# S5 taps side by side in DRAM, chunk tokens numbered backwards, gate loads pinned, GLU operand cast earlier, in a one-core encoder layer on Trainium2

## The chip, the cores and the metric

The kernel runs on one core of one Trainium2 chip, as one launch. The metric is the device time of an execution in microseconds; lower is better. The kernel before was run three times and took 880.37, 882.69 and 883.11 us (median 882.69).

## The reference

One encoder layer over 512 tokens of width 1024, all in float32. The part that matters here is the mixer: a projection feeds an S5 state-space branch (bidirectional, 32 groups of 16 channels with 64 states each) and a gMLP branch, and both are merged by sigmoid gates. Memory attention and a SwiGLU feed-forward layer follow.

```python
def s5_branch(xa, lam_re, lam_im, log_step, b_re, b_im, c_re, c_im, d, w_glu):
    u = xa.astype(f32).reshape(bsz, seq, S5_GROUPS, S5_GROUP).transpose(1, 0, 2, 3)
    y = d.astype(f32).reshape(S5_GROUPS, S5_GROUP) * u
    for direction, reverse in ((0, False), (1, True)):
        y = y + s5_scan(u, ..., reverse)
    y = jax.nn.gelu(y.transpose(1, 0, 2, 3).reshape(bsz, seq, S5_WIDTH))
    y = y * jax.nn.sigmoid(y @ w_glu.astype(f32))
    return y.astype(xa.dtype)

def reference(...):
    memn = rms_norm(mem, mem_norm_g)
    n = rms_norm(h, mix_norm_g[i])
    proj = n @ w_in[i]
    ya = s5_branch(xa, ...)
    yb = sgu_branch(zu, zv, ...)
    merged = gate_a * (ya @ w_proj_a[i]) + gate_b * (yb @ w_proj_b[i])
    h = h + merged @ w_out[i]
    h = h + memory_cross_attention(...)
    h = h + swiglu(...)
    return rms_norm(h, final_norm_g)
```

## The kernel before

**Matmuls in three parts.** A float32 product is made of three fp32r matmuls: each operand is split into a high part (a cast on ScalarE, line 85) and a low part (a subtraction on VectorE, line 86). `feat`, `tokm` and `product` (line 1143) run these; `feat` and `tokm` go through `mm3` (line 358). Weights come in blocks of 512 KB by a written-out plan: a block is loaded on the SyncE queue three blocks ahead (`wraw`), split two ahead (`whi`, `wlo`), and each of the three buffers exists three times. So the load of a block waits until the block three places ahead of it has been split, and the split until the block three places ahead of it has been multiplied.

**Side work.** The S5 branch is a generator, `s5_program`, that is advanced by `tick` between the matmul blocks of the main work; `later(n, fn)` puts a step off. `finish_side` runs out what is left of it. After recording, a scheduler orders each engine's instructions by a simulated timeline; instructions wrapped in `in_order` keep their program order among each other.

**S5.** The 512 tokens are 64 chunks of Q = 8 tokens. Within a chunk the result is a convolution with 15 lags, from 7 ahead to 7 behind; between chunks a scan over 64 states carries on. The groups are worked off in four octets o of GO = 8 groups. `s5_kernels(o)` makes the taps: `products` multiplies them on TensorE (pk), `store` copies them from PSUM to `ks` and adds the skip term, `spill` writes them to DRAM (`kd`, one row of 15 x 16 values for each group and input channel; four DMAs on SyncE, four on GpSimd), and `load` reads them back as the matrix `tt` (line 855), one DMA for each of the eight tokens l of a chunk, on the partitions l, l + 8, and so on. For the octets 2 and 3 the state matrices e are spilled too (`ed`) and `reload` (line 861) brings both back as soon as octet o - 2 has released the buffers. `s5_outputs(o)` then multiplies: for each group one matmul with the taps (py<-tt,u) and two with the states (py<-e,ss), line 941; `emit` copies the result (yn), `turn_y` transposes it (pyt), and `put` applies GELU (y, line 962) and stores it to DRAM (`yd`, line 965). There is one buffer for y.

**The end of the mixer.** While the octets end, the main work multiplies the second gate (its sigmoids go to `part`, line 1171) and then the gMLP projection by w_proj_b as 14 block products of a seven-product scheme (`b_product`, lines 1208 to 1243; names bx, bv, bq, x1, v1). `seed` (qv, line 1156) copies a product into a second PSUM bank, and the next product is added there; `kept` (u, line 1161) saves one before it is added to. After the last block product, `finish_side` ends S5 and closes its pool; a new pool holds the GLU's operand: `ygt` is loaded from `yd` (line 1255), cast (`yg_hi`, line 1256) and subtracted (`yg_lo`, line 1257). Two `feat` blocks multiply it by w_glu; `glu_evac` takes the sigmoid and multiplies (glu, line 1265) and splits into `ya`. The gains g_mem and g_x (line 471) and the gates `gat` (line 1279, four loads of 512 KB from `gad`, three buffers) are loaded next, and four `feat` blocks multiply `ya` by w_proj_a; `pa_evac` multiplies by the gate and adds `part`. Every load named here is issued by SyncE, in one queue, in order: a load that waits holds those behind it.

Of the kernel before, what the change touches and what calls it, by code (L numbers as in the profile page):

```python
# [9 lines left out]
F32 = mybir.dt.float32  # L10
F32R = mybir.dt.float32r
AF = mybir.ActivationFunctionType
ALU = mybir.AluOpType
# [39 lines left out]
def hybrid_layer_kernel(  # L53
# [566 lines left out]
    def s5_setup():  # L620
# [89 lines left out]
        for src in (pr, pi):  # L710
            pe = s5p.tile([P, G, Q], F32, name="pe%d" % len(st["pe"]))
            pw = s5p.tile([P, G, Q], F32, name="pw%d" % len(st["pw"]))
            A_.copy(pe[lo_], src[lo_, :, 0:Q])
            V.tensor_copy(pe[hi_], src[hi_, :, 0:Q][:, :, ::-1])
            V.tensor_copy(pw[lo_], src[lo_, :, 1:Q + 1][:, :, ::-1])
            A_.copy(pw[hi_], src[hi_, :, 1:Q + 1])
            st["pe"].append(pe)
            st["pw"].append(pw)
        ca = s5p.tile([P, 2, G], F32, name="ca")
# [55 lines left out]
    def lc(t, g):  # L775
        return t[:, g].rearrange("p a b -> p (a b)")
# [4 lines left out]
    def s5_kernels(o):  # L781
# [43 lines left out]
            later(0.5, lambda: store(ps))  # L825

        def store(ps):
            ks = s5p.tile([P, 2, P], F32, tag="y", name="ks")
            dd = s5p.tile([P, 2, C], F32, tag="dd", name="dd", bufs=2)
            in_order(V.tensor_tensor(dd, st["dmask"].unsqueeze(1).to_broadcast([P, 2, C]),  # L830
                                     st["dcol"][:, 2 * o:2 * o + 2].unsqueeze(2).to_broadcast([P, 2, C]), ALU.mult))
            nc.scalar.copy(ks, ps)
            V.tensor_tensor(ks[:, :, 0:C], ks[:, :, 0:C], dd, ALU.add)
            later(0.5, lambda: spill(ks))

        def spill(ks):
# [12 lines left out]
    ed = {o: dp.tile([2, P, GO * Q * C], F32, name=f"ed{o}") for o in (2, 3)}  # L849

    def load(o, es):
        tt = s5p.tile([P, GO, P], F32, tag=("tt", "raw_c")[o % 2], name="tt")
        kf = st["kd", o].rearrange("g c l e -> c g (l e)")
        for l in range(Q):
            nc.sync.dma_start(tt[l::Q], kf[:, :, (7 - l) * C:(15 - l) * C])  # L855
        st["oct", o] = (es[0], es[1], tt)

    def reload(o):
# [60 lines left out]
    def s5_outputs(o):  # L919
# [12 lines left out]
        def mix_():  # L932
            ps = aux("py", (P, 4, 2, 4, C))
            ks = (0, 1, 2) if o in ed else (1, 2, 0)
            for h in range(4):
                for k in ks:
                    for j in range(2):
                        g = 4 * j + h
                        a = u[:, o * GO + g, :] if k == 0 else ss[:, k - 1, g, :]
                        b = (tt[:, g, :], lc(e_re, g), lc(e_im, g))[k]  # L940
                        in_order(nc.tensor.matmul(ps[64 * j:64 * j + 64, :, :, h, :].rearrange("p q d c -> p d q c"), a,
                                                  b.rearrange("p (d q c) -> p d q c", d=2, q=4),
                                                  start=k == ks[0], stop=k == ks[2], tile_position=(0, 64 * j)))
            later(1, lambda: emit(ps))
            if o + 2 in ed:
                later(0.5, lambda: reload(o + 2))
# [283 lines left out]
    b_product(x1, 1, 6)  # L1230
    u1 = zf[0][:, :, T0]
    nc.scalar.copy(u1, x1)
    b_product(bq, 0, 3)
    gated(0, 1, T0, minus(bq, u2))
    b_product(x1, 1, 7)
    u3 = kept(x1, "u3")
    bq = unit_bank("bq")
    b_product(bq, 1, 5, True)
    gated(1, 1, T1, minus(bq, u3))
    b_product(x1, 1, 4)  # L1240
    gated(1, 0, T1, x1)
    b_product(bq, 1, 3)
    gated(1, 1, T0, minus(bq, u1))
    finish_side()
    s5.close()
    mgx = ExitStack()
# [7 lines left out]
    for m in range(4):  # L1254
        nc.sync.dma_start(ygt[:, m, :], yd[m].rearrange("p l n -> p (l n)"))
        in_order(nc.scalar.copy(yg_hi[:, m, :], ygt[:, m, :]))
        nc.vector.tensor_tensor(yg_lo[:, m, :], ygt[:, m, :], yg_hi[:, m, :].bitcast(F32), ALU.subtract)
    ya_hi = mgp.tile([P, 4, T], F32R, name="ya_hi")
    ya_lo = mgp.tile([P, 4, T], F32R, name="ya_lo")

# [15 lines left out]
    gat = {}  # L1276
    for c in range(KD // 2):
        gat[c] = mgp.tile([P, 2, T], F32, tag="gat", name="gat", bufs=3)
        nc.sync.dma_start(gat[c], gad[2 * c:2 * c + 2].rearrange("m p t -> p m t"))

    def pa_evac(m, j, ps):
        z = np_.tile([P, T], F32, tag="ev", name="mg", bufs=2)
# [560 lines left out]
```

## Time and profile before

| | us |
|---|---|
| median of the runs | 882.69 |
| the profiled execution, its own time | 879.7 |
| its span, first to last instruction | 877.8 |
| TensorE matmuls (PE) busy | 863.7 |
| TensorE weight loads (PEld) busy | 768.2 |
| VectorE (DVE) busy | 658.0 |
| ScalarE (ACT) busy | 465.0 |
| GpSimd (POOL) busy | 87.1 |

PE's clock stays at full speed in all 40 slices of the page. In the views of the profile a row of a timeline gives the start and the length in us, the engine, the line of the kernel, the operation, what is written and read (out<-in), the shape, and in brackets the engine's idle time ahead of it and what ended it. SPq is the SyncE queue that issues DMAs. A wait row gives who waited for whom, the total in us, how often and the longest. Starts of matmuls lie closer together than their lengths, since they are pipelined.

### The profile page before, as it was taken

The page shows a single profiled execution, that of the slowest core. Times are in us where ns is not written, and L with a number is a line of the kernel's source. Part 1 is how long each engine was busy: PE and PEld are TensorE (multiplying, and loading weights), DVE is VectorE, ACT ScalarE, POOL GpSimd, SP SyncE. Part 2 cuts the span into 40 slices and gives each one's busy share as a digit, 9 for nine tenths or more (in the row PEclk, how much of TensorE's full clock was granted, in tenths as well). Part 3 has the DMA queues.
Part 4 walks back from the last instruction along what each step waited for, and adds up shares of the span by engine and source line. Part 5 has one row for each costly group of instructions (what it writes and reads, how often), then busy time and mean ns, then how long its engine had stood idle before and what let it go on. Part 6 is the DMA issues. An engine that isn't in the chain of part 4 may idle for free.

```text
span 877.8 us, 14762 instructions
## 1 busy us (share of the span) xinstructions
PE 863.7 (98%) x5760; PEld 768.2 (88%) x5760; DVE 658.0 (75%) x1068; ACT 465.0 (53%) x690; POOL 87.1 (10%) x117
## 2 busy tenths in 40 slices
PE   9999999999999999999999999999999999999996
PEld 6788888888888988889899878999999999988875
DVE  5699796899845677569757746767878767899875
ACT  5644863244375453447556545645555455656664
POOL 1001201211000010110001001101111111000010
PEclk9999999999999999999999999999999999999999
DMA  8769565798656896724579645547899898366572
GB/s 254 199 188 280 103 192 146 159 259 194 166 180 187 284 259 195 264 94 160 203 227 263 160 123 157 153 132 172 222 238 229 213 236 218 97 188 207 193 237 99
DMA packets 119816, 169.56 MB, mean 193 GB/s; under 512 B 9521, under 2 KB 85057, under 8 KB 119618
## 3 DMA queue, kind: packets, MB, share of 16 engines
q1 hardware_dynamic: 100162, 141.64, 49.1%
q0 software_dynamic: 19296, 26.45, 19.3%
q8 instruction: 45, 0.74, 0.3%
q10 hardware_dynamic: 288, 0.52, 0.2%
q14 instruction: 25, 0.20, 0.1%
HBM read 159.71 MB, written 48.73 MB: 237 GB/s over the span
## 4 chain that ended last, share of the span: by engine, by line
PE 90%; DMA 4%; SPq 2%; DVE 1%; issue 1%; ACT 1%; POOL 0%; POOLq 0%; ACTq 0%; DVEq 0%
PE pf L358 24%; PE pt L358 17%; PE px L1143 12%; PE dx L358 7%; PE pq L1143 6%; PE dq L358 3%; PE pv L1143 3%; PE qx L1143 2%; PE dv L358 2%; PE pz L886 1%; PE psc L358 1%; PE qq L1143 1%; PE ptr L520 1%; PE po L358 1%; DMA slab<-in_s_log_step_dram 1%; SPq L855 1%
## 5 line engine op out<-in xcount | busy, mean ns | idle before, releaser
L85 ACT CAST whi<-wraw 128x1024 fp32r<-128x1024 f32 (+1 forms) x145 | 148.6, 1025 | 150.8 <-PE pf L358 43.0
L86 DVE TENSOR_TENSOR wlo<-wraw,whi 128x1024 fp32r<-128x1024 f32 (+1 forms) x145 | 172.2, 1188 | 73.4 <-ACT whi L85 72.3
L358 PE MATMUL pf<-xn,whi 128*128 128x512 f32 x448 | 140.0, 392 | 0.0
L358 PEld LDWEIGHTS pf<-xn,whi 128*128 128x128 f32 x448 | 83.7, 188 | 17.2 <-issue 0.2
L358 PE MATMUL pf<-xn,wlo 128*128 128x512 f32 x224 | 87.7, 392 | 0.0
L1143 PE MATMUL px<-fn,whi 128*128 128x256 f32 x480 | 83.4, 277 | 0.0
L1143 PEld LDWEIGHTS px<-fn,whi 128*128 128x128 f32 x480 | 72.7, 188 | 0.2
L86 DVE TENSOR_TENSOR wlo<-b,whi 128x1024 fp32r<-128x1024 f32 x40 | 48.9, 1222 | 27.1 <-ACT whi L85 27.1
L85 ACT CAST whi<-b 128x1024 fp32r<-128x1024 f32 x40 | 42.2, 1054 | 50.6 <-PE px L1143 27.7
L1143 PE MATMUL px<-fn,wlo 128*128 128x256 f32 x240 | 66.4, 277 | 0.0
L1143 PE MATMUL pq<-s,whi 128*128 128x256 f32 x320 | 55.1, 276 | 0.0
L358 PE MATMUL dx<-whi,s 128*128 128x512 f32 x170 | 53.4, 390 | 0.4 <-DVE h L1768 0.4
L86 DVE TENSOR_TENSOR wlo<-t,whi 128x1024 fp32r<-128x1024 f32 x30 | 36.7, 1224 | 19.4 <-ACT whi L85 19.4
L85 ACT CAST whi<-t 128x1024 fp32r<-128x1024 f32 x30 | 31.6, 1054 | 35.3 <-PE pv L1143 12.4
L358 PEld LDWEIGHTS pf<-xn,wlo 128*128 128x128 f32 x224 | 42.1, 188 | 8.9 <-issue 0.2
L1143 PEld LDWEIGHTS pq<-s,whi 128*128 128x128 f32 x320 | 48.3, 188 | 0.0
L1143 PEld LDWEIGHTS px<-fn,wlo 128*128 128x128 f32 x240 | 45.1, 188 | 0.0
L358 PE MATMUL pt<-whi,xn 128*128 128x512 f32 x128 | 44.0, 411 | 0.8 <-ACT xn L85 0.8
L1143 PE MATMUL pq<-s,wlo 128*128 128x256 f32 x160 | 44.2, 276 | 0.0
L358 PEld LDWEIGHTS dx<-whi,s 128*128 128x128 f32 x170 | 31.8, 188 | 7.5 <-issue 0.8
L358 PE MATMUL dx<-wlo,s 128*128 128x512 f32 x85 | 32.9, 389 | 0.0
L358 PEld LDWEIGHTS pt<-whi,xn 128*128 128x128 f32 x128 | 24.4, 193 | 6.5 <-ACT xn L85 1.5
(451 smaller groups left out, 2198.2 us busy)
## 6 DMA issues: line engine op xcount, KB each, us to landing
wraw<-in_w_in_dram SPq DMA_DIRECT2D x36, 512.0 KB, 4.7
dsum<-in_w_down_dram SPq DMA_DIRECT2D x20, 512.0 KB, 5.6
wraw<-dsum SPq DMA_DIRECT2D x20, 512.0 KB, 4.2
b<-in_w_gate_dram SPq DMA_DIRECT2D x15, 512.0 KB, 5.7
b<-in_w_up_dram SPq DMA_DIRECT2D x15, 512.0 KB, 5.7
wraw<-in_w_down_dram SPq DMA_DIRECT2D x15, 512.0 KB, 4.4
dsum<-in_w_down_dram POOLq DMA_DIRECT2D x10, 512.0 KB, 7.3
dsum<-dsum POOLq DMA_DIRECT2D x10, 512.0 KB, 7.8
```

The costliest lines, as they stand in the source:

```text
L85: hi = nc.scalar.copy(dst_hi, src)
L86: lo = nc.vector.tensor_tensor(dst_lo, src, dst_hi.bitcast(F32), ALU.subtract)
L358: m = nc.tensor.matmul(ps, a[x], b[y], start=start and i == 0, stop=stop and i == 2, skip_group_check=free)
L520: nc.tensor.transpose(ps[:, j, :], src[:, k * P:(k + 1) * P], ident)
L855: nc.sync.dma_start(tt[l::Q], kf[:, :, (7 - l) * C:(15 - l) * C])
L886: nc.tensor.matmul(ps[:, g, :], wt[:, g, :], u[:, o * GO + g, :], start=True, stop=True)
L1143: nc.tensor.matmul(ps[:, j, :], a[x], b[y], start=start and j == k == i == 0, stop=k == 3 and i == 2, skip_group_check=True)
```

## The change

It consists of four parts. (1) In DRAM the taps of an octet are kept by pairs of groups: a row holds for each lag the values of two groups side by side (`kd` is 4 x 16 x 15 x 32). `store` writes `ks` in that order, each of the eight spill DMAs writes contiguous rows, and `load` is four DMAs on 128 partitions with rows of 1 KB instead of eight on 16 partitions with rows of 512 B; its source is a written-out access pattern whose rows overlap, one lag further for each token. The matmuls read the taps with a step. (2) So that the lag grows with the partition, the tokens of a chunk are numbered backwards: `xa_evac` and the powers `pw` are reversed. (3) The gate loads are wrapped in `in_order`. (4) `finish_side`, the closing of the S5 pool and the load, cast and subtraction of the GLU operand stand ahead of the last five block products instead of behind them.

```diff
@@ -712,8 +712,8 @@
             pw = s5p.tile([P, G, Q], F32, name="pw%d" % len(st["pw"]))
             A_.copy(pe[lo_], src[lo_, :, 0:Q])
             V.tensor_copy(pe[hi_], src[hi_, :, 0:Q][:, :, ::-1])
-            V.tensor_copy(pw[lo_], src[lo_, :, 1:Q + 1][:, :, ::-1])
-            A_.copy(pw[hi_], src[hi_, :, 1:Q + 1])
+            V.tensor_copy(pw[lo_], src[lo_, :, 1:Q + 1])
+            A_.copy(pw[hi_], src[hi_, :, 1:Q + 1][:, :, ::-1])
             st["pe"].append(pe)
             st["pw"].append(pw)
         ca = s5p.tile([P, 2, G], F32, name="ca")
@@ -825,20 +825,21 @@
             later(0.5, lambda: store(ps))
 
         def store(ps):
-            ks = s5p.tile([P, 2, P], F32, tag="y", name="ks")
+            ks = s5p.tile([P, Q, 2, C], F32, tag="y", name="ks")
             dd = s5p.tile([P, 2, C], F32, tag="dd", name="dd", bufs=2)
             in_order(V.tensor_tensor(dd, st["dmask"].unsqueeze(1).to_broadcast([P, 2, C]),
                                      st["dcol"][:, 2 * o:2 * o + 2].unsqueeze(2).to_broadcast([P, 2, C]), ALU.mult))
-            nc.scalar.copy(ks, ps)
-            V.tensor_tensor(ks[:, :, 0:C], ks[:, :, 0:C], dd, ALU.add)
+            nc.scalar.copy(ks.rearrange("p l q e -> p q l e"), ps.rearrange("p q (l e) -> p q l e", e=C))
+            V.tensor_tensor(ks[:, 0], ks[:, 0], dd, ALU.add)
             later(0.5, lambda: spill(ks))
 
         def spill(ks):
-            kd = dp.tile([GO, C, 15, C], F32, name=f"kd{o}")
+            kd = dp.tile([4, C, 15, 2 * C], F32, name=f"kd{o}")
+            rows = ks.rearrange("p l q e -> p (l q e)")
+            taps = kd.rearrange("j c l e -> j c (l e)")
             for j in range(4):
-                kdj = kd.rearrange("(q j) c l e -> j c q (l e)", j=4)[j]
-                nc.sync.dma_start(kdj[:, :, 7 * C:15 * C], ks[32 * j:32 * j + C])
-                nc.gpsimd.dma_start(kdj[:, :, 0:7 * C], ks[32 * j + C:32 * j + 2 * C, :, 0:7 * C])
+                nc.sync.dma_start(taps[j][:, 14 * C:], rows[32 * j:32 * j + C])
+                nc.gpsimd.dma_start(taps[j][:, 0:14 * C], rows[32 * j + C:32 * j + 2 * C, 0:14 * C])
             st["kd", o] = kd
             if o not in ed:
                 later(1.2, lambda: load(o, es))
@@ -849,10 +850,12 @@
     ed = {o: dp.tile([2, P, GO * Q * C], F32, name=f"ed{o}") for o in (2, 3)}
 
     def load(o, es):
-        tt = s5p.tile([P, GO, P], F32, tag=("tt", "raw_c")[o % 2], name="tt")
-        kf = st["kd", o].rearrange("g c l e -> c g (l e)")
-        for l in range(Q):
-            nc.sync.dma_start(tt[l::Q], kf[:, :, (7 - l) * C:(15 - l) * C])
+        tt = s5p.tile([P, 4, 2 * P], F32, tag=("tt", "raw_c")[o % 2], name="tt")
+        taps = st["kd", o].rearrange("j c l e -> j c (l e)")
+        for j in range(4):
+            t = taps[j]
+            nc.sync.dma_start(tt[:, j], type(t)(t.tensor, t.offset, [t.ap[0], (2 * C, Q), (1, 2 * P)],
+                                                dep_tracking_offset=t.dep_tracking_offset))
         st["oct", o] = (es[0], es[1], tt)
 
     def reload(o):
@@ -937,10 +940,10 @@
                     for j in range(2):
                         g = 4 * j + h
                         a = u[:, o * GO + g, :] if k == 0 else ss[:, k - 1, g, :]
-                        b = (tt[:, g, :], lc(e_re, g), lc(e_im, g))[k]
+                        b = (lc(e_re, g), lc(e_im, g))[k - 1].rearrange("p (d q c) -> p d q c", d=2, q=4) if k else \
+                            tt[:, h].rearrange("p (d q j c) -> p j d q c", d=2, q=4, j=2)[:, j]
                         in_order(nc.tensor.matmul(ps[64 * j:64 * j + 64, :, :, h, :].rearrange("p q d c -> p d q c"), a,
-                                                  b.rearrange("p (d q c) -> p d q c", d=2, q=4),
-                                                  start=k == ks[0], stop=k == ks[2], tile_position=(0, 64 * j)))
+                                                  b, start=k == ks[0], stop=k == ks[2], tile_position=(0, 64 * j)))
             later(1, lambda: emit(ps))
             if o + 2 in ed:
                 later(0.5, lambda: reload(o + 2))
@@ -1019,7 +1022,7 @@
 
     def xa_evac(m, j, ps):
         xa = np_.tile([P, Q, NCH], F32, tag="ev", name="xa", bufs=2)
-        nc.scalar.copy(xa, ps.rearrange("p (n l) -> p l n", l=Q))
+        nc.scalar.copy(xa, ps.rearrange("p (n l) -> p l n", l=Q)[:, ::-1, :])
         nc.sync.dma_start(ud[m * P:(m + 1) * P], xa)
 
     for c0 in range(0, SW, 256):
@@ -1230,6 +1233,20 @@
     b_product(x1, 1, 6)
     u1 = zf[0][:, :, T0]
     nc.scalar.copy(u1, x1)
+    finish_side()
+    s5.close()
+    mgx = ExitStack()
+    mgp = mgx.enter_context(tc.tile_pool(name="merge", bufs=1))
+    align(mgp)
+
+
+    yg_hi = mgp.tile([P, 4, T], F32R, name="yg_hi")
+    yg_lo = mgp.tile([P, 4, T], F32R, name="yg_lo")
+    ygt = mgp.tile([P, 4, T], F32, name="ygt")
+    for m in range(4):
+        nc.sync.dma_start(ygt[:, m, :], yd[m].rearrange("p l n -> p (l n)"))
+        in_order(nc.scalar.copy(yg_hi[:, m, :], ygt[:, m, :]))
+        nc.vector.tensor_tensor(yg_lo[:, m, :], ygt[:, m, :], yg_hi[:, m, :].bitcast(F32), ALU.subtract)
     b_product(bq, 0, 3)
     gated(0, 1, T0, minus(bq, u2))
     b_product(x1, 1, 7)
@@ -1241,20 +1258,6 @@
     gated(1, 0, T1, x1)
     b_product(bq, 1, 3)
     gated(1, 1, T0, minus(bq, u1))
-    finish_side()
-    s5.close()
-    mgx = ExitStack()
-    mgp = mgx.enter_context(tc.tile_pool(name="merge", bufs=1))
-    align(mgp)
-
-
-    yg_hi = mgp.tile([P, 4, T], F32R, name="yg_hi")
-    yg_lo = mgp.tile([P, 4, T], F32R, name="yg_lo")
-    ygt = mgp.tile([P, 4, T], F32, name="ygt")
-    for m in range(4):
-        nc.sync.dma_start(ygt[:, m, :], yd[m].rearrange("p l n -> p (l n)"))
-        in_order(nc.scalar.copy(yg_hi[:, m, :], ygt[:, m, :]))
-        nc.vector.tensor_tensor(yg_lo[:, m, :], ygt[:, m, :], yg_hi[:, m, :].bitcast(F32), ALU.subtract)
     ya_hi = mgp.tile([P, 4, T], F32R, name="ya_hi")
     ya_lo = mgp.tile([P, 4, T], F32R, name="ya_lo")
 
@@ -1276,7 +1279,7 @@
     gat = {}
     for c in range(KD // 2):
         gat[c] = mgp.tile([P, 2, T], F32, tag="gat", name="gat", bufs=3)
-        nc.sync.dma_start(gat[c], gad[2 * c:2 * c + 2].rearrange("m p t -> p m t"))
+        in_order(nc.sync.dma_start(gat[c], gad[2 * c:2 * c + 2].rearrange("m p t -> p m t")))
 
     def pa_evac(m, j, ps):
         z = np_.tile([P, T], F32, tag="ev", name="mg", bufs=2)
```

More of the change, by code (lines that the diff above doesn't have):

```diff
@@ L1232, in hybrid_layer_kernel @@
     nc.scalar.copy(u1, x1)
[L1233 to L1243, printed above, removed]
     finish_side()
@@ L1257, in hybrid_layer_kernel @@
         nc.vector.tensor_tensor(yg_lo[:, m, :], ygt[:, m, :], yg_hi[:, m, :].bitcast(F32), ALU.subtract)
+    b_product(bq, 0, 3)
+    gated(0, 1, T0, minus(bq, u2))
+    b_product(x1, 1, 7)
+    u3 = kept(x1, "u3")
+    bq = unit_bank("bq")
+    b_product(bq, 1, 5, True)
+    gated(1, 1, T1, minus(bq, u3))
+    b_product(x1, 1, 4)
+    gated(1, 0, T1, x1)
+    b_product(bq, 1, 3)
+    gated(1, 1, T0, minus(bq, u1))
     ya_hi = mgp.tile([P, 4, T], F32R, name="ya_hi")
```

## The prediction

> **What bounds the kernel now.** I read the page first, for the engine that is never idle, then the chain of waits, then the view of waits on TensorE, to see how much of its time could be saved at all.
>
> ```profile
> span 877.8 us, 14762 instructions
> PE 863.7 (98%) x5760; PEld 768.2 (88%) x5760; DVE 658.0 (75%) x1068; ACT 465.0 (53%) x690; POOL 87.1 (10%) x117
> PE 90%; DMA 4%; SPq 2%; DVE 1%; issue 1%; ACT 1%; POOL 0%; POOLq 0%; ACTq 0%; DVEq 0%
> ```
>
> TensorE is busy for 863.7 of 877.8 us. The edit neither adds nor removes a matmul: the S5 outputs keep their 64 matmuls with the taps and 128 with the states, of the same shapes. So the ceiling of any gain is the 14.1 us in which TensorE stands still, and of these only the part that lies where the edit works.
>
> ```profile
> PE py L941 <- issue: 1.7, 1, 1.7
> PE bq L1143 <- DVE wlo L86: 0.8, 1, 0.8
> PE pf L358 <- DVE glu L1265: 0.3, 1, 0.3
> ```
>
> These are three of the eight waits of TensorE that the view lists (in total, times, longest), and all three lie in the stretch from 250 to 325 us that the edit rearranges: the S5 output matmuls (py), a block product (bq), and the start of the projection behind the GLU (pf). The SyncE queue in order of time (start, length, instruction, count) shows what is late for the first two:
>
> ```profile
> 251.14 0.81 SPq L861 DMA_DIRECT2D e<-ed  x2
> 252.05 5.84 SPq L855 DMA_DIRECT2D tt<-kd  x8
> 258.00 0.99 SPq L861 DMA_DIRECT2D e<-ed  x2
> 259.43 5.83 SPq L855 DMA_DIRECT2D tt<-kd  x8
> 265.36 1.29 SPq L965 DMA_DIRECT2D yd<-y  x2
> 276.58 0.39 SPq L224 DMA_DIRECT2D wraw<-in_w_proj_b_dram  x1
> 278.20 1.23 SPq L965 DMA_DIRECT2D yd<-y  x2
> 281.37 1.75 SPq L1255 DMA_DIRECT2D ygt<-yd  x4
> 284.14 2.14 SPq L1279 DMA_DIRECT2D gat<-gad  x2
> 286.38 0.82 SPq L224 DMA_DIRECT2D wraw<-in_w_proj_b_dram  x1
> ```
>
> Eight tap loads take 5.84 us of the queue, 0.73 us each, and there are two such groups in a row, with two state loads ahead of each. The chain of waits (start, length) carries this on:
>
> ```profile
> 263.23 2.92 DMA tt<-kd
> 266.15 1.23 issue
> 286.38 8.67 DMA wraw<-in_w_proj_b_dram
> 296.23 1.24 DVE wlo L86
> ```
>
> A tap load that was issued at 263.23 needed 2.92 us to land, and one more stood behind it. And the weight block issued at 286.38, right behind the gate loads (gat), needed 8.67 us, which ends in the 1.24 us split (wlo) that the product bq waits for. TensorE itself in order of time:
>
> ```profile
> 261.42 0.39 PE L358 MATMUL pf<-xn,wlo 128*128 128x512 f32 x1
> 261.64 0.28 PE L1143 MATMUL bx<-yb_hi,whi 128*128 128x256 f32 x1
> 267.38 0.44 PE L941 MATMUL py<-tt,u 128*64 128x128 f32 x4 [1.74 <-issue]
> 270.15 0.38 PE L1143 MATMUL bx<-yb_lo,whi 128*128 128x256 f32 x1
> 270.37 0.28 PE L1143 MATMUL bx<-yb_hi,wlo 128*128 128x256 f32 x1
> 276.40 0.28 PE L1143 MATMUL qv<-yb_hi,whi 128*128 128x256 f32 x1
> 322.17 0.39 PE L358 MATMUL pf<-yg_hi,wlo 128*128 128x512 f32 x1
> 323.33 0.50 PE L358 MATMUL pf<-ya_hi,whi 128*128 128x512 f32 x1 [0.32 <-DVE glu L1265]
> 323.85 0.50 PE L358 MATMUL pf<-ya_lo,whi 128*128 128x512 f32 x1
> ```
>
> The wait ahead of the fourth octet's py is 1.74 us. Matmuls overlap, so their price is the distance of their starts: 261.64 - 261.42 = 0.22 us for one of 512 columns.
>
> **The change part by part, and the sum.** The sum is made against the profiled execution: span 877.8 us, own time 879.7 us, which lies 3.0 us under the median of the runs shown, 882.69.
>
> *Tap loads.* Sixteen issues of 64 KB become eight of 128 KB in this stretch, with the same bytes. At 0.73 us each (a row with the same 128 pieces in it; the piece is twice as long) the queue runs: states to 251.95, four taps to 255.0, states to 256.0, and after the same pause of 0.4 us as before 258.99 to 259.43 four taps from 256.4 to 259.4. The last is issued at 258.7 and, with 2.92 us, lands at 261.6. When will TensorE ask? In the built program's order the third octet's py now stands eleven 512-column matmuls earlier, and the fourth directly behind it and one transpose group. So 261.64 - 11 x 0.227 = 259.1 for the third, and with 2.8 us of py and 0.4 of transposes 262.3 for the fourth. The margin is 0.7 us. Against it stands the traffic:
>
> ```profile
> 252.00:254.00 2.00, 2.00 (x40) 1.91 (x36) 1.18 (x2) 1.39 (x1) 0.55 (x1) 1.00 0.84 248
> 254.00:256.00 2.00, 2.00 (x15) 1.65 (x12) 1.75 (x2) 1.97 (x1) 1.07 (x2) 1.00 0.97 356
> 288.00:292.00 4.00, 4.00 (x36) 4.00 (x36) 1.39 (x2) 1.28 (x2) 0.00 (x0) 1.00 1.03 397
> ```
>
> (the last two columns are the busy share of the DMA engines and GB/s.) Four state tiles of 128x1024 f32 and two tap tiles of the same size are 3.1 MB; from 251.1 they last at 356 GB/s until 259.9, at 248 until 263.8. So the fourth py waits between 0 and 1.5 us. I take 0.3, near the quick end, because longer pieces and a free queue are nearer to the 356 row: -1.4 (bounds -1.74 and -0.2). The skill has a rule against this: the Trainium skill, DMA: Bandwidth & Descriptors, section Bandwidth, puts the limit of a core on its HBM at about 358 GB/s, so that fewer issues help only until that is reached. By that figure alone the loads end at 259.8, an estimate, and the sum stays; the 397 GB/s of the last row is over it, with stores counted in.
>
> *Order around py.* A lone block product between py groups costs 270.37 - 270.15 = 0.22 instead of 0.12 us. The new order drops two such changes of kind: -0.2 (0 to -0.4).
>
> *Gate loads pinned.* They now follow the two gain loads, behind the GLU weights. 1.5 MB leave the 281 to 293 us stretch, where the DMA engines run at 1.03. The block that took 8.67 us is to take the 4 us of its kind, so its split ends over 3 us earlier and the 0.8 us wait goes: -0.8 (0 to -0.8). The gates then are loaded near 310 us and first read after the first projection chunk, about 328 us; that is 18 us of cover for loads that took under 9 us in the thickest traffic. If that cover went, the evacuation would hold a PSUM bank and TensorE would stand for what is missing. I put it at 0.
>
> *GLU operand early.* The four casts and four subtractions now run between block products, while their split operands lie three products ahead. Before, both GLU chunks were interleaved because their operand came late, so all four results came at once and the projection stood: 0.32 us in the row, and 323.85 - 323.33 = 0.52 against 0.23 in the next step, so 0.6 in all. In the new order the chunks run one after the other, and three of the four results are ready when the projection starts: -0.6 (0 to -0.6).
>
> *Setup and spill.* The reversed copies keep their sizes and engines' loads; the spill sends the same bytes in the same eight issues. The tap loads of the first two octets fall from 16 to 8, at 158 to 174 us, where TensorE runs on w_in blocks without a wait. Taken at 0; without that cover a block could come 1 us later.
>
> *ScalarE and its waits.* This is what speaks against. The order on ScalarE now puts a GELU (y, L962) between the two last sigmoids of the gate, with four operand casts and the last sigmoid behind it.
>
> ```profile
> L962 ACT ACT_TABLE_LOAD  x2: 1283/1283/1283, 256.1 to 268.7; - x2
>   DMA yd<-y: 5.3, 2
> 257.35 0.60 ACT L962 ACTIVATE y<-pyt 128x512 f32<-128x512 f32 x1
> 257.84 1.04 ACT L85 CAST whi<-wraw 128x1024 fp32r<-128x1024 f32 x1
> 261.62 2.18 ACT L85 CAST s<-zf 128x512 fp32r<-128x512 f32 x4 [0.82 <-PE pf L358]
> 275.19 0.59 ACT L1156 COPY qv<-bx 128x512 f32<-128x512 f32 x1
> 275.01 2.46 DMA yd<-y
> ```
>
> Two table loads more, 2 x 1.28 us, and each y waits for the store of the one before (5.3 us of ScalarE's idle time already). Behind that y wait the casts, the last gate sigmoid, two weight casts, the next y and the copy qv. The first store's second half is issued 0.65 us (half of 1.29) behind 259.4 and lands 2.46 us later, at 262.5, when the transposes that this y reads are done too. From there 1.28 + 0.6 + 2.18 + 1.28 + 0.6 + 1.04 + 1.28 + 0.6 + 1.04 + 0.59 = 10.5 us, less nine overlaps of about 0.1 (257.35 + 0.60 against 257.84): qv is done at 272.1 to 273.0. Its product started at 276.40, and by -1.4 - 0.2 would start at 274.8. The slack is 1.8 us or more: 0. The upper bound is +1.0, since a later copy (u) stands behind a weight cast whose load went out ahead of the last store (276.58 against 278.20) and now follows it. The Trainium skill, ScalarE: Activation LUTs, section What ACT_TABLE_LOAD costs, counts 2.66 us for a switch, with a drain. By it the chain is an estimated 4 us longer and qv would stop TensorE by 2 to 3 us. The trace doesn't bear the drain out: the y at 257.35 starts 1.3 us after its 1283 ns load at 256.1.
>
> Sum: -1.4 - 0.2 - 0.8 - 0.6 = -3.0, so 876.7 for a profiled execution and 882.69 - 3.0 = 879.7 for the median; I write 879.6.
>
> **The rivals.** *Bandwidth, not issues.* The taps land no earlier than bytes allow, and the wait stays 1.5 us. For it: 0.97 busy at 254. Against: only 0.84 in the window ahead of it. Sum -0.2 - 0.2 - 0.8 - 0.6 = -1.8: 880.9.
>
> *The stall goes elsewhere.* The split and the GLU waits go, but the copies behind weight casts cost 1.0, or the projection still stands 0.6 behind ScalarE. Sum -3.0 + 1.6 = -1.4: 881.3. For it: ScalarE takes its work in order, and its slack is 1 to 2 us. Against: it is busy for only 53% of the span.
>
> *Slower: the store in the way of ScalarE.* Place: the second y, waiting for the first store. It decides once that store lands later than 264.3, the 262.5 and the slack of 1.8. If it lands as slowly as the weight block did (8.67 us, here behind 3.1 MB of states and taps), from 260.05, that is 268.7; this y is done at 270.6, the casts and the sigmoid behind it at 275.3; its own store, at 5.6 us (the middle of 2.46 and 8.67) from 271.2, lands at 276.8; load, y, cast and copy take 3.5 more, so qv is done at 280.3, and TensorE stands 280.3 - 274.8 = 5.5 us. Sum -3.0 + 5.5 = +2.5, and 0.3 for the wait of the store's weight block behind it in the queue: 885.5. For it: the 5.3 us row. Against: stores of this kind landed in 2.46 us.
>
> *The change doesn't do what it says*: the pinned gates hold the last projection block, which is now queued behind them, and the projection waits instead of bq. Its load would go out near 312, and its product starts 72 matmuls of 0.227 behind the projection's start, near 335; at 8.67 us it is there at 321. It would give 880.5, and I fold it into the second rival.
>
> **How the numbers follow.** Forecast 0.56 (own range 877.5 to 881), bandwidth 0.13, stall elsewhere 0.13, slower 0.18. A measurement of this kernel tells about 0.3% (2.65 us) from no change: the lines are 880.0 and 885.3. The forecast lies under the lower one, the two mild rivals between them, the slower one over the upper: faster 0.56, same 0.26, slower 0.18. The forecast's margin to its line is only 0.4 us and the runs shown scatter by 2.7, but it is as likely to come out lower as higher, and of the mild rivals some would pass the line the other way. The range: down to -3.5 (all three waits whole, both changes of order) with 2.7 of scatter, 876.5; up to the second rival's 881.3 with the 2.3 by which the lowest run lies off the median, 883.6. It leaves the slower case out.
>
> **What would show it right or wrong.** Right: tap loads in fours of about 2.9 us on the SyncE queue; no idle time ahead of py near 262 or under 0.5; the gate loads behind g_x; no wait of bq for wlo; the GLU's results in single file and no wait for glu. Wrong: TensorE idle ahead of qv or of bx behind a copy u; ScalarE's wait for yd<-y grown well over 5.3 us; or new waits between 325 and 440 us, where the built order also shuffles the output projection and the attention's norms, which I price at 0 for want of a wait seen there. A slower matmul with the strided taps would show as more than 0.22 us between starts of py groups.

## The result, and the profile after

| | before | after |
|---|---|---|
| median of 22 runs each, us | 882.94 | 879.0 |
| lowest and highest, us | 878.67, 887.06 | 877.45, 884.41 |
| profiled execution, its own time, us | 879.7 | 883.48 |

After over before: 0.9966, 95% interval 0.995 to 0.9981. A second comparison, the first of the experiments, gave 0.9986 (0.9971 to 1.0). The two intervals overlap only between 0.9971 and 0.9981, which would be a gain of 1.7 to 2.6 us. The predicted time, 879.6, was met; its terms were not all met, and most of the experiments are about that.

The page of the profiled execution after has this to set against the lines of before:

```profile
span 881.7 us, 14747 instructions
PE 863.3 (98%) x5760; PEld 769.7 (87%) x5760; DVE 658.4 (75%) x1068; ACT 467.2 (53%) x692; POOL 86.4 (10%) x117
PEclk8999999999999999999999999999999999999999
```

This is one of the slower executions of its 22. The 8 at the head of the clock line lies in the first 22 us, ahead of everything that the edit touches. A second profile of the same kernel (the run whole_again, 878.79 us, span 877.0) is nearer the median, and I use it where times are compared. The waits of TensorE (total, times, longest), first in the profile after:

```profile
PE qv L1146 <- ACT qv L1159: 1.9, 1, 1.9
PE py L945 <- DMA tt<-kd: 1.5, 1, 1.5
```

and in the run whole_again:

```profile
PE qv L1146 <- ACT qv L1159: 1.9, 1, 1.9
PE py L945 <- DMA tt<-kd: 1.3, 1, 1.3
PE bx L1146 <- ACT u L1164: 0.9, 1, 0.9
```

The waits for wlo at bq and for glu at pf, 0.8 and 0.3 us before, are in neither list. The wait at py is hardly shorter. Two new ones, 1.9 and 0.9 us, stand behind copies of ScalarE. The SyncE queue of the profile after shows what became of the tap loads:

```profile
252.75 0.81 SPq L864 DMA_DIRECT2D e<-ed  x2
253.66 3.16 SPq L857 DMA_DIRECT2D tt<-kd  x4
256.92 1.46 SPq L864 DMA_DIRECT2D e<-ed  x2
258.48 3.11 SPq L857 DMA_DIRECT2D tt<-kd  x4
317.12 2.30 SPq L1282 DMA_DIRECT2D gat<-gad  x3
```

Eight issues of some 0.78 us take the place of sixteen, as forecast, and the gate loads are at 317 instead of 284 us. But the queue's end is not the landing. The view of transfers (count, KB each, median us from issue to landing), for 246 to 266 us, of the kernel before:

```profile
e<-ed SPq DMA_DIRECT2D x4, 512.0 KB, 4.4
tt<-kd SPq DMA_DIRECT2D x16, 64.0 KB, 3.0
```

and of the run whole_again:

```profile
e<-ed SPq DMA_DIRECT2D x4, 512.0 KB, 6.5
tt<-kd SPq DMA_DIRECT2D x8, 128.0 KB, 6.1
yd<-y SPq DMA_DIRECT2D x2, 128.0 KB, 5.2
```

The same bytes, issued faster, took twice as long from issue to landing. The chain of waits of the profile after leads from there to the wait at qv:

```profile
258.48 7.13 DMA tt<-kd
265.74 2.84 PE py L945 x48
268.58 2.54 PE pf L358 x10
271.14 0.97 ACT s L85 x2
273.35 1.28 ACT L1174
275.13 1.04 ACT whi L85
276.19 1.28 ACT L965
277.49 0.60 ACT y L965
278.08 0.93 ACT whi L85
279.02 0.50 ACT qv L1159
279.56 4.56 PE qv L1146 x24
```

The first of the last octet's four tap loads (issued at 258.48) holds the last py, behind it come the last matmuls of the gate block (pf), and only then may ScalarE cast s: the kernel puts s in the place of xn, which the gate block still reads. Two table loads (L1174, L965) stand on the way to the copy qv.

### The profile page after: what moved, and what is told of

Read it like the earlier page. It is cut to its first block, busy times and chain, and to the rows that moved or that the text cites. A ratio compares the mean times of both kernels' runs of the same rounds, so it can differ in the third digit from the quotient of the medians.

```text
span 881.7 us, 14747 instructions
## 1 busy us (share of the span) xinstructions
PE 863.3 (98%) x5760; PEld 769.7 (87%) x5760; DVE 658.4 (75%) x1068; ACT 467.2 (53%) x692; POOL 86.4 (10%) x117
## 4 chain that ended last, share of the span: by engine, by line
PE 91%; DMA 4%; ACT 2%; DVE 2%; SPq 1%; issue 1%; POOL 0%; POOLq 0%; ACTq 0%; DVEq 0%
PE pf L358 26%; PE pt L358 17%; PE px L1146 12%; PE pq L1146 6%; PE dx L358 5%; PE dq L358 3%; PE pv L1146 3%; PE bx L1146 2%; PE qx L1146 2%; PE dv L358 2%; PE pz L889 2%; PE ptr L520 1%; PE po L358 1%; PE qv L1146 1%; DMA slab<-in_s_log_step_dram 1%; DMA wraw<-qsum 1%
```

## The experiments

Each row is set against runs of the kernel before on the same chip; waits at py (for tt, as far as the profile tells) and at the first qv are those of the run's profile, in us.

| run | median us | before us | ratio and 95% interval | py | qv |
|---|---|---|---|---|---|
| whole_again | 880.04 | 881.0 | 0.9986 (0.9971 to 1.0) | 1.3 | 1.9 |
| taps_only | 881.75 | 881.0 | 1.0012 (0.9995 to 1.0029) | 0.8 | 1.9 |
| gates_only | 880.61 | 881.0 | 0.999 (0.9976 to 1.0005) | 1.5 | 0 |
| glu_only | 878.91 | 881.0 | 0.9977 (0.9964 to 0.999) | 2.9 | 0 |
| gates_glu | 879.7 | 881.37 | 0.9981 (0.9966 to 0.9995) | 1.7 | 0 |
| y_alt | 880.44 | 881.37 | 0.9992 (0.9981 to 1.0004) | 0.6 | 1.9 |
| tt2_early | 878.17 | 881.37 | 0.9955 (0.9941 to 0.9969) | 0 | 0.5 |
| no_e | 877.81 | 881.37 | 0.996 (0.9946 to 0.9975) | 0.2 | 0.5 |
| pf_pinned | 876.52 | 880.67 | 0.9949 (0.9931 to 0.9968) | 0 | 0 |
| gg_pinned | 875.77 | 880.67 | 0.9945 (0.9925 to 0.9965) | 0 | 0 |
| tables_paired | 882.9 | 880.67 | 1.0022 (1.0003 to 1.004) | 2.1 | 0.5 |
| taps_in_halves | 881.37 | 880.67 | 1.0007 (0.9993 to 1.0021) | 0.7 | 2.9 |

**The whole and its parts.** The whole change once more:

> The changed kernel once more, for a second profile of it. Theory W (the three waits, as predicted): it is about 3 us faster than before (ratio near 0.9965), and a typical profile shows py waiting for taps for 0 to 0.5 us. Rival B (bytes, not issues): py still waits 1 us or more for tt<-kd, and qv stands behind a late store for 1 to 2 us, as in the first profile, so the gain must come from somewhere else.

The taps and the numbering alone, that is the change with the two small parts undone (the lines from `finish_side()` to the subtraction of `yg_lo` behind the last block products again, and this):

```diff
-        in_order(nc.sync.dma_start(gat[c], gad[2 * c:2 * c + 2].rearrange("m p t -> p m t")))
+        nc.sync.dma_start(gat[c], gad[2 * c:2 * c + 2].rearrange("m p t -> p m t"))
```

> Only the taps' layout and the reversed numbering; gates not pinned, GLU operand behind the last block products. Theory W: -1.6 us against before (-1.4 for the py wait, -0.2 for order). Rival B: within 0.5 us of before, or slower by up to 1 us, since the py wait stays near 1.5 us and the qv wait of 1 to 2 us comes on top; the bq wait of 0.8 us may move or vanish behind it.

In the kernel before, the gate loads alone:

```diff
-        nc.sync.dma_start(gat[c], gad[2 * c:2 * c + 2].rearrange("m p t -> p m t"))
+        in_order(nc.sync.dma_start(gat[c], gad[2 * c:2 * c + 2].rearrange("m p t -> p m t")))
```

> Only the gate loads wrapped in in_order. Theory W: -0.8 us against before, no wait of bq for wlo. Rival B (the gain lies here): -1.5 to -3 us, because in most executions the blocks behind the gate loads land later than in the one profile of before.

And in the kernel before the GLU's move alone, the last but one part of the change's diff:

```diff
+    finish_side()
...
+        nc.vector.tensor_tensor(yg_lo[:, m, :], ygt[:, m, :], yg_hi[:, m, :].bitcast(F32), ALU.subtract)
     b_product(bq, 0, 3)
```

> Only the GLU operand's load, cast and subtraction ahead of the last five block products; gates not pinned. Theory W: -0.6 us against before, no wait of pf for glu; the wait of bq for wlo stays at 0.8 us or grows, since the gate loads stay where they are. Rival B: -1 us or more.

The largest edit brings no gain: 1.0012 with an interval that holds 1, as its rival had it. Of the two small parts only the GLU's move is clear of noise by itself, and at 2.1 us it is worth more than the 0.6 expected; that of the gates, 0.999, has 1 in its interval. The whole, too, came out nearer to its rival than to the 3 us expected. The profile of taps_only has both new waits and both old ones that the small parts remove:

```profile
PE qv L1146 <- ACT qv L1159: 1.9, 1, 1.9
PE bx L1146 <- ACT u L1164: 1.0, 1, 1.0
PE py L945 <- DMA tt<-kd: 0.8, 1, 0.8
PE bx L1146 <- DVE wlo L86: 0.8, 1, 0.8
PE pf L358 <- DVE glu L1268: 0.3, 1, 0.3
```

So the tap part takes about 1 us off py and puts 2.9 us on two copies. The wait for wlo falls only where the gates are pinned (absent in gates_only), or nearly so with the GLU's move (0.3 in glu_only); the wait for glu falls only with the GLU's move.

**Both small parts, without the taps.** The edits of gates_only and glu_only in one kernel:

> The kernel before with the gate loads pinned and the GLU operand cast early; the taps stay as they were. Theory (the two waits add, and the tap layout earns nothing): no bq wait for wlo and no pf wait for glu, so 0.8 + 0.6 = 1.4 us less than before, ratio 0.9975 to 0.9985, and no qv wait of 1.9 us, since ScalarE runs both last gate sigmoids back to back as before; about 1 us faster than the whole change. Rival (the tap layout is worth what the prediction said, 1.4 us): slower than the whole change by 1 us or more, with a py wait for tt above 1.5 us that the whole change has not.

No wait at qv, no wlo and no glu wait, 1.7 at py. The ratio, 0.9981, is the one expected. But it is level with the whole change, not 1 us better as I had it for certain: the intervals overlap. These runs show no gain of the taps on top of the two. That the two parts simply add up is not shown either; glu_only alone did as well.

**Is it the store?** My first reading was the one of the prediction's slower rival: in the profile after, ScalarE stood 5.2 us at the second y, waiting for the store yd, and everything behind it was late.

```profile
267.60 1.28 ACT L965 ACT_TABLE_LOAD   x1 [5.20 <-DMA yd<-y]
```

So y got a second place:

```diff
-            y = s5p.tile([P, 512], F32, tag="y", name="y")
+            y = s5p.tile([P, 512], F32, tag=("y", "raw_b")[o % 2], name="y")
```

> The whole change, with the buffer of the GELU's result taken in turn from two places, so that the second octet's y no longer waits for the first store yd. Theory (the qv wait of 1.9 us and the u wait of 0.9 us come from ScalarE standing 5.2 us until that store lands, with the sigmoid, the copies and the weight casts behind it): ScalarE's wait for yd at the second y goes from 5.2 us to under 1, the qv wait from 1.9 to under 0.5, and the time falls by 1.5 to 2.5 us against the whole change, ratio to before 0.996 to 0.997. Rival (ScalarE's amount of work and its table loads make the lag, not the store): qv still waits over 1.2 us, and the time stays within 0.5 us of the whole change.

ScalarE in order of time in this run (start, length, instruction, idle time ahead of it and what ended it):

```profile
265.81 0.60 ACT L965 ACTIVATE y<-pyt 128x512 f32<-128x512 f32 x1 [0.61 <-PE pyt L960]
271.74 2.18 ACT L85 CAST s<-zf 128x512 fp32r<-128x512 f32 x4 [5.33 <-PE pf L358]
273.94 1.28 ACT L1174 ACT_TABLE_LOAD   x1
275.24 0.60 ACT L1174 ACTIVATE part<-pf 128x512 f32<-128x512 f32 x1
279.51 0.59 ACT L1159 COPY qv<-bx 128x512 f32<-128x512 f32 x1
```

The wait for the store is gone (0.61, and for the transposes), and the 5.33 us of idle time stand one instruction later, ahead of s, where they end with the gate block pf. qv still makes TensorE wait 1.9 us, and a later qv 1.6. My theory fell. The place that decides is the end of the gate block: from the start of s to the end of qv ScalarE needs 279.51 + 0.59 - 271.74 = 8.4 us, and TensorE has only its block products bx and bq in the meantime.

**One table load less.** Here the sigmoids of the gate and the y GELUs are kept in program order, on top of y_alt:

```diff
-            nc.scalar.activation(y, ps.rearrange("p s q n -> p (s q n)"), AF.Gelu_apprx_tanh)
+            in_order(nc.scalar.activation(y, ps.rearrange("p s q n -> p (s q n)"), AF.Gelu_apprx_tanh))
...
-        nc.scalar.activation(part[:, m - OFF_GB // P, :], ps, AF.Sigmoid)
+        in_order(nc.scalar.activation(part[:, m - OFF_GB // P, :], ps, AF.Sigmoid))
```

> The run y_alt (two buffers for y in turn), with the gate's sigmoids and the y GELUs kept in program order on ScalarE: the second y stands ahead of both last sigmoids, so that two table loads fall away and none stands between the casts s and the last sigmoid. TensorE's order is nearly that of the whole change. Theory (the qv wait is the end of the gate block plus ScalarE's chain behind it, in which one table load is 1.28 us): the first qv wait goes from 1.9 to about 0.6 us, and the time falls by 1 to 1.5 us against the run y_alt. Rival (ScalarE is late by its weight casts or its loads): qv still waits over 1.2 us.

The first qv wait came out as expected, the time as the opposite. The profile:

```profile
265.99 0.69 PE L945 MATMUL py<-tt,u 128*64 128x128 f32 x4 [2.06 <-DMA tt<-kd]
280.01 0.39 PE L1146 MATMUL qv<-yb_hi,whi 128*128 128x256 f32 x1 [0.46 <-ACT qv L1159]
294.49 0.39 PE L1146 MATMUL qv<-yb_hi,whi 128*128 128x256 f32 x1 [3.01 <-ACT qv L1159]
```

The chain behind pf is one table load shorter, and the first qv waits 0.46 instead of 1.9: that mechanism holds. But py stood 2.06 us, at half the clock for some 3 us behind it (see the last section), and a second qv waits 3.0 us. In y_alt and here two of the four loads ygt<-yd stand on SyncE ahead of the weight block that the cast ahead of the second qv needs (issued at 286.76 and 286.49); in whole_again that block goes out ahead of them (at 281.83). ScalarE waits 4.49 us for it in this run. Why py waited longer here than in y_alt stays open.

**Bytes or issues?** Three runs on when the taps land. First, the third octet's taps loaded ahead with those of the first two:

```diff
-            if o not in ed:
+            if o != 3:
                 later(1.2, lambda: load(o, es))
...
-        tt = s5p.tile([P, 4, 2 * P], F32, tag=("tt", "raw_c")[o % 2], name="tt")
+        tt = s5p.tile([P, 4, 2 * P], F32, tag=("tt", "raw_c", "raw_b", "raw_c")[o], name="tt")
...
-        load(o, es)
+        if o == 3:
+            load(o, es)
+        st["oct", o] = (es[0], es[1], st["tt", o])
```

> The whole change, with the third octet's taps loaded ahead, with those of the first two, so that the two bursts of late loads hold 2.6 MB in place of 3.1 and SyncE issues four transfers less there. Theory (bytes set when the taps land): the last octet's py wait for tt goes from 1.3 us to 0.3 to 0.8, its transfers land in 5 us or less in place of 6 to 7, and the first store yd lands 1 to 1.5 us earlier; time 0.5 to 1.5 us under the whole change. Rival (each transfer's own time from issue to landing sets it, whatever else is on the way): landings of 6 to 7 us and a py wait of 1.3 us or more stay.

Second, no reload of the spilled states:

```diff
-        es = [s5p.tile([P, GO, Q, C], F32, tag="e%d" % i, name="e%d" % i, bufs=2) for i in range(2)]
-        for i, e in enumerate(es):
-            nc.sync.dma_start(glc(e), ed[o][i])
-        load(o, es)
+        load(o, st["oct", o - 2][:2])
```

> The whole change without the late reload of the spilled states of octets 2 and 3 (2 MB); their products use the states of octets 0 and 1, so the output differs there. Theory (the taps share the bandwidth with these states): tt lands 2 to 3.5 us after its issue in place of 5.5 to 7, no py wait for tt is over 0.3 us, the first store yd lands in 2 to 3 us in place of 5.1, and with it the qv wait falls from 1.9 to under 1; time 1.5 to 3 us under the whole change. Rival (the new layout's long rows, overlapping eight times in the source, are slow by themselves): tt still lands 5 us or more after its issue, with the state loads gone.

Third, each tap load in two halves:

```diff
-            nc.sync.dma_start(tt[:, j], type(t)(t.tensor, t.offset, [t.ap[0], (2 * C, Q), (1, 2 * P)],
-                                                dep_tracking_offset=t.dep_tracking_offset))
+            for q in range(2):
+                nc.sync.dma_start(tt[64 * q:64 * q + 64, j],
+                                  type(t)(t.tensor, t.offset + 8 * q * t.ap[0][0], [(t.ap[0][0], 8), (2 * C, Q), (1, 2 * P)],
+                                          dep_tracking_offset=t.dep_tracking_offset))
```

> The whole change, with each tap load cut in two of 64 partitions: the same bytes and rows in twice the issues, as many as before the change. Theory (bytes set when the taps land, not issues): the last octet's last tap load lands within 1 us of that of the whole change, counted from the first state load; three matmuls of the gate block (0.7 us) stand between the two py now, so the py wait for tt goes from 1.3 us to 0.5 to 1.5, and the time stays within 0.7 us of the whole change. Rival (the prediction's: issues set it): the last tap load lands 2 us or more later, and py waits 2.5 us or more.

The view of transfers of the run no_e:

```profile
tt<-kd SPq DMA_DIRECT2D x8, 128.0 KB, 2.9
yd<-y SPq DMA_DIRECT2D x4, 128.0 KB, 2.5
```

and the stretch from 260 to 264 us (the last three columns are granted clock, busy share of the DMA engines, GB/s) in whole_again:

```profile
260.00:264.00 4.00, 2.71 (x44) 2.33 (x42) 0.69 (x1) 0.28 (x1) 0.00 (x0) 1.00 1.07 303
```

With the states gone, the same eight loads with the same overlapping rows land in 2.9 us instead of 6.1, and the wait at py is 0.2. So the new rows are not slow by themselves; with the states on the way the DMA engines are full, at 303 GB/s. Full engines are not the whole of it, though. The trace counts sixteen completions for each load. Of the load that py waits for in whole_again, fifteen had come by 262.04 and the sixteenth came at 263.31, while TensorE was ready at 262.15: nearly all of the 1.3 us there is the last of sixteen. In y_alt the last came 0.1 us behind the fifteenth. Why one lags is not shown.

tt2_early gains more than the 0.5 to 1.5 us expected: 0.9955 against 0.9986 for the whole change, or 2.7 us. There is no wait for tt at all, and of the two table loads behind s that of the sigmoid falls away as in no_e, so that qv waits 0.5. The wait at u stays in both, 0.8 and 1.0 us. The last loads of tt2_early still took 5.6 us in the median, not under 5 as I expected. In both runs the scheduler also moved more of the gate block behind the last py (19 and 24 matmuls), so not all of their gain need come from the landing.

taps_in_halves tests the prediction's issues. SyncE issues as many loads as before the change. Its first state load, and the start of the last octet's py in TensorE's order of time:

```profile
251.32 0.81 SPq L866 DMA_DIRECT2D e<-ed  x2
```

```profile
264.30 0.44 PE L947 MATMUL py<-tt,u 128*64 128x128 f32 x4 [0.75 <-DMA tt<-kd]
```

The same two in whole_again:

```profile
250.62 0.81 SPq L864 DMA_DIRECT2D e<-ed  x2
```

```profile
263.44 0.44 PE L945 MATMUL py<-tt,u 128*64 128x128 f32 x4 [1.29 <-DMA tt<-kd]
```

From the one to the other it is 13.0 us in halves, 12.8 us in the whole change, and 267.38 - 251.14 = 16.2 us before it. Doubling the issues moved that start by 0.2 us, so their count doesn't set it. But that start is not the last landing. A load now holds whole pairs of groups, so that the first matmuls of py need one load in four, where before each load held one token of every group and the first matmul needed all eight. The third and fourth quarter of py in halves start at

```profile
265.64 0.42 PE L947 MATMUL py<-tt,u 128*64 128x128 f32 x4
266.63 0.44 PE L947 MATMUL py<-tt,u 128*64 128x128 f32 x4
```

that is 0.99 us apart, where the quarters before are 0.66 to 0.68 apart: the fourth waits for the last half load. By the trace's completions that load was issued 12.6 us behind the first state load (at 263.94) and landed 15.2 us behind it (266.50). In the whole change the last load landed after 14.2 us (264.79), before it after 15.9 (267.07). So the issues do show in the last landing. And of the 3.4 us by which py starts earlier in the whole change than before it, counted from the first state load, 1.8 are the earlier landing; the rest is that the first load is enough to begin.

Nor does the run change the count of issues alone: the trace has eight late completions for each half and sixteen for each whole load, so that a half was probably carried by fewer DMA engines. And it took 1.8 us longer than the whole change by the ratios, where I had expected at most 0.7: its first qv waits 2.9 us, with half the clock behind it (see the last section).

**The order itself.** Between the two layouts the scheduler also moved the last gate block. Before, both parts of it stand ahead of the last two py; after, eleven of its matmuls stand behind the last py. Here they are held in place, and py of octets 2 and 3 is recorded a step later:

```diff
-            if turn:
+            if turn or side.get("pin"):
                 in_order(m)
...
+        side["pin"] = c0 + 256 == D
         feat(w_in, OFF_GB + c0, xn, KD, gb_evac)
+    side["pin"] = False
...
-        later(1, mix_)
+        later(2 if o >= 2 else 1, mix_)
```

> The whole change, with the last gate blocks' matmuls (pf) kept in program order and py of octets 2 and 3 recorded one step later: on TensorE half of the last gate block stands ahead of each of the two py, and the first block product with its copy qv comes ahead of the third octet's GELU. Nothing else is changed. Theory (the taps land about 2 us earlier than before, but the new order also sends TensorE to py over 3 us earlier, and it ends the gate block so late that ScalarE's casts, tables and the copy qv follow late): no py wait for tt over 0.3 us, no qv wait over 0.3 us, and the time falls by 2 to 3 us against the whole change, ratio to before 0.995 to 0.9965. Rival (the waits only move on to the next copies, u, or to wlo): waits of 1.5 us or more in all appear between 270 and 300 us, and the time stays within 1 us of the whole change.

And the same edit in gates_glu, that is in the old tap layout:

> The kernel before with gate loads pinned and the GLU operand early, in the old tap layout, and the same pinning of the last gate blocks as in the run pf_pinned. Theory (the tap layout earns nothing once TensorE has other work in front of py): no py wait for tt over 0.5 us, time within 0.5 us of the run pf_pinned. Rival (the eight shorter issues still land too late): a py wait of 1 us or more, and 1 us or more slower than pf_pinned.

In pf_pinned TensorE's list of waits between 250 and 330 us is empty but for 0.4 us at a transpose, whose row is the first here; the second shows the taps' landing:

```profile
PE pyt L960 <- DVE yn L954: 0.4, 1, 0.4
tt<-kd SPq DMA_DIRECT2D x8, 128.0 KB, 6.6
```

The taps land as slowly as ever, 6.6 us, and ScalarE stands 4.85 us for the store yd, and neither costs anything: half of the gate block lies ahead of each py, and the block product and qv come ahead of the third y and its table load. The gain over the whole change is 880.04 - 876.52 = 3.5 us across two sets of runs, by the ratios 0.0037 x 881 = 3.3, a little over the 2 to 3 expected. The pinning and the later step were not tried one by one. In the old layout the same order does as well: 0.9945 against 0.9949, and no wait at py, with loads of 3.5 us in the median. Both are clear of the kernel before. Against the whole change their intervals lie below that of whole_again (0.9971 and up) but overlap that of the first comparison (0.995 to 0.9981). The tap layout is worth nothing measurable in them.

## Why the prediction was right in its sum, and where it was wrong

*Gate loads pinned, -0.8.* The mechanism was right: the wait for wlo is there in taps_only (0.8) and in before, and in no run with the pin at this place. The size is not resolved by the time of gates_only. TensorE waits nowhere for the gates at their new place, though one of them took 12.0 us to land in whole_again, where the prediction had under 9.

*GLU operand early, -0.6.* The mechanism was right, the size too small. The stretch from the first matmul of the projection to the first of the attention's queries, in before:

```profile
322.40 0.61 PE L358 MATMUL pf<-ya_hi,whi 128*128 128x512 f32 x2
441.84 0.40 PE L1143 MATMUL qq<-hse,whi 128*128 128x256 f32 x2
```

and in whole_again:

```profile
322.04 0.39 PE L358 MATMUL pf<-ya_hi,whi 128*128 128x512 f32 x1
439.87 0.40 PE L1146 MATMUL qq<-hse,whi 128*128 128x256 f32 x2
```

is 119.44 us in one and 117.83 in the other: 1.6 us, not 0.6. Of the parts, glu_only has the short stretch (117.5), gates_only and taps_only the long one (119.4 and 119.5); all eleven profiles with the move have 117.5 to 117.8. The wait for glu and the slow steps around it are part of it; the rest lies behind, in stretches that the prediction priced at 0 for want of a wait seen there.

*Tap loads, -1.4.* This is the step that failed first. The issue times were right: the last tap load was to go out 7.6 us behind the first state load (258.7 - 251.14), and in whole_again it went out 8.1 us behind (at 258.70). The 2.92 us to land, from a row of before, were wrong: in whole_again that load landed 6.1 us behind its issue. The row came from a queue that issued slowly enough for the DMA engines to keep up, as taps_in_halves suggests: with as many issues its last load landed 2.6 us behind its issue. The prediction also took the last load for the one that py waits for, but py begins on the first of the four, which landed 6.8 us behind its issue, at 263.31. The taps did arrive earlier than before, but TensorE came earlier too (at 262.15 in whole_again, 263.44 - 1.29, foreseen for 262.3), so the wait fell from 1.7 to 1.3 where the prediction had 0.3. The rival called bandwidth, not issues, came nearest in this term, with 1.5. The matmuls with strided taps are not slower: the first two rows of py start 0.24 us apart in whole_again (263.44 and 263.68) and in before (267.38 and 267.62).

*ScalarE and its waits, 0.* This is the step that failed most: +1.9 at qv, +0.9 at u. The prediction counted ScalarE's chain of 10.5 us correctly, piece by piece, but started it at the first store, with a slack of 1.8 us. The store was later than thought (265.3 in whole_again, not 262.5, and past the 264.3 of the slower rival), yet y_alt shows that this was not what decided. (It can be: in taps_in_halves the store held s about 1 us beyond the gate block's end, and qv waited 2.9 us.) Nor did a switch of tables cost more than its load: in y_alt's rows the sigmoid at 275.24 starts 1.30 us behind the load at 273.94. The chain starts at the end of the gate block, and the prediction had itself noted that the last py moved ahead of eleven matmuls of it. It used that for TensorE's arrival and not for ScalarE's start. The 0.9 at u is the upper bound of this term, +1.0, at the place given for it: the copy behind a weight cast whose load now follows the last store.

*The sum.* -0.4 at py, -0.8 at bq, -1.6 behind the GLU, +1.9 and +0.9 at the copies make 0.0; the two profiles differ by 0.8 us (877.8 and 877.0) and the medians by 1.0 in one comparison and 3.9 in the other. The list of waits doesn't carry the whole: by it the projection would start 1.6 us later than in before, and by the rows above it starts 0.36 earlier. Of the difference 0.56 lie ahead of all this (the first matmul on w_in starts at 41.50 instead of 42.06), and most of the rest in steps between block products that no wait lists. So idle time was not the ceiling that the prediction took it for. Behind the queries whole_again is 1.2 us longer (877.0 - 439.87 against 877.8 - 441.84), in a part that the edit leaves alone. The term for the order around py, -0.2, was not measured by itself. So a forecast of -3.0 came near the measured time partly by luck, that is by errors that cancel: two terms of 1 and 2.8 us too good, one of 1 us too bad, and a session in which the difference came out at the wide end. What makes up the rest of the 3.9 stays open.

## What to carry to other kernels

When an edit issues the same bytes faster, price the landing by what is in flight then, not by a row from a queue that was slow: here 3.0 us became 6.1. When the order moves, follow each moved group into every engine that waits for it; here eleven matmuls behind a load were worth more than the load. A wait for data can be cured by the work that is put in front of it: the same order removed it in both layouts.

## What the runs showed of the hardware

A wait of TensorE of about 2 us can cost twice. In the profile after, the 1.85 us at qv are followed by this stretch, the matmuls being granted 0.58 of the clock:

```profile
280.00:284.00 4.00, 4.00 (x24) 4.00 (x23) 2.71 (x4) 2.10 (x4) 0.00 (x0) 0.58 0.76 197
```

That is 0.42 x 4 = 1.7 us more. In whole_again the same wait, 1.87 us, left the clock at 1.00:

```profile
280.00:284.00 4.00, 4.00 (x38) 4.00 (x37) 3.01 (x4) 1.91 (x3) 0.14 (x1) 1.00 0.69 195
```

24 matmuls fit in the one stretch and 38 in the other. Over all profiles, in the stretch of the edit, the clock fell to half after waits of 1.85 us (after), 2.06 (tables_paired), 2.9 (glu_only) and 2.9 (taps_in_halves, where it stayed there for some 6.8 us), and not after any wait up to 1.74, after 1.87 in three runs, or after 3.01 (tables_paired, the second qv). So two executions of one kernel may differ by this alone, and a wait of 2 us or more may be worth more than it shows. The Trainium skill, TensorE: Matmul & The Clock Gate, section What's actually happening, puts the fall to half rate behind an idle window of about 3.4 us, free-running; that waits of one length end either way fits such a window, but the waits that were enough here are shorter than it.
